# A gated delta rule layer in a four-layer trunk: decays by ScalarE, masks and key scaling moved in the queues, sums of squares by TensorE

## The chip, the cores and the metric

The kernel runs on one core of a Trainium2 chip. The metric is the device time of one execution in microseconds, from the launch of the program to its end. Before the change it was 1247.69 us, the median of three runs (1246.97 to 1249.37).

Five engines work side by side, each with a queue of its own that it serves in order: TensorE (PE, matrix products; its weight loads are listed as PEld), VectorE (DVE), ScalarE (ACT), GpSimd (POOL) and SyncE (SP), which here only issues transfers. Products land in PSUM, in banks of 128 rows by 512 numbers; everything else lives in SBUF, 128 partitions wide.

## What is computed

The reference is a decoder trunk of four layers for one sequence of 256 tokens with 1024 features. Every layer is `x += mixer(rmsnorm(x)); x += conv_ffn(rmsnorm(x))`. The mixers are, in order, block-sparse attention, a short gated convolution, a gated delta rule and attention again. The change touches the third alone, with 8 heads of 128. In short:

```python
qkv = silu(causal_dwconv(proj[..., :3 * d], conv_w))
q, k = l2norm(q) * dh ** -0.5, l2norm(k)
gc = cumsum(g)                                 # g <= 0, so gc only falls
decay = where(i >= j, exp(gc[i] - gc[j]), 0)
a_mat = where(i > j, (k_beta @ k.T) * decay, 0)
t_mat = inverse(a_mat + eye)                   # unit lower triangular
u, w = t_mat @ v_beta, t_mat @ (k_beta * exp(gc))
attn = where(i >= j, (q @ k.T) * decay, 0)
v_new = u - w @ state
o = (q * exp(gc)) @ state + attn @ v_new
state = state * exp(g_last) + (k * exp(g_last - gc)).T @ v_new
```

The reference cuts the sequence into chunks of 64; the kernel uses two chunks of 128 tokens (t = 0 and 1), which is the same in exact arithmetic. Where i >= j the difference gc[i] - gc[j] is minus the distance of the two, so exp(-|gc[i] - gc[j]|) is the decay there, and a number between 0 and 1 on the other side of the diagonal.

## The kernel before

**Weights.** All weights come as one stream of 400 chunks of 512 KB, each eight tiles of 128x128. `Stream` issues a chunk's transfer on SyncE's queue into one of four buffers (wraw, L130); ScalarE rounds it to the high part (whi, L152), VectorE takes the rest (wlo, L153), five chunks ahead of TensorE. A tile's product is three matmuls of 256 columns (xh by whi, xl by whi, xh by wlo). The transfer of a chunk is issued in the program right after the conversion of an earlier one, so SyncE's queue waits wherever a buffer is still to be read.

**The order of TensorE.** It is written by a planner, `Weave`. `fill()` yields the products of the layer job by job (here q0 to q7, one query and one key tile of a head each, then values and gates), and beside it steps are registered: generators that yield `(cost, wait)`. The planner keeps a time t of its own; it advances by the cost of what is emitted, and a step goes on when its wait, a number or a named event with a lag, is past. All the lags are constants (L_QK = 6.0, L_BLOCKS = 6.0, L_JOIN = 13.0 and so on, in the planner's microseconds). TensorE's instructions stay in the order in which the planner emits them. The other engines' queues are ordered by a scheduler that estimates when each instruction can run; `after(inst)` pins an instruction behind the TensorE instruction emitted last.

**The delta rule layer** (`gdn`). The heads are two halves of four; half 0 is ready first. In the program's order:

- `gates` makes g, its running sum gc (L665), and calls `decays` for both halves. `decays` (L681) gets gc[i] in every row by TensorE into a bank of PSUM, subtracts gc[j] and adds a mask of 0 or -1e30 on VectorE (L692, 16 times 128x128), and takes exp of the whole on ScalarE (L696, twice 128x1024): s.dt.
- `queries_keys` (L699) is there for each head: VectorE scales the job's bank (u, L702), ScalarE makes the first tap of the convolution (L420) and VectorE the other three (L422), each for the query and the key, and ScalarE the silu (L707).
- `lengths` (L711), for each head of a half: TensorE transposes query and key of both chunks into one bank (four transposes, L257), ScalarE copies the key's first chunk out (kt, L724) and squares all four out of the bank, each with a sum along the row (jk, L729). Then few-column work on VectorE and GpSimd makes the factors rn, sk and sw, and VectorE scales kt (L742).
- `systems` (L745): TensorE multiplies key by key and key by query, VectorE multiplies with sk and s.dt into aq (L758, two for each head). SyncE stores the key part in DRAM (L766), and VectorE makes am, aq with the off-diagonal 16-blocks alone (L772).
- `invert` (L775): SyncE gathers the diagonal 16x16 blocks (bl, L781), GpSimd inverts them by elimination, 28 small instructions in a row (L792, L794), SyncE stores the result (L796) and gathers it back in another layout (xc, L799); VectorE makes xt32 (xt, L802).
- `join16` and `join_half` put the inverse together from the 16-blocks: a transpose on VectorE (xi, L809), products with am, and so on up to 128. Then the states and outputs of the two chunks follow (`half`, L940).

"Group" below means TensorE's instructions of one head in `lengths`; "key product" means a head's two products in `systems`.

## Time and profile before

| what | before |
|---|---|
| median of three runs | 1247.69 us (1246.97 to 1249.37) |
| the profiled execution, device time | 1247.2 us |
| its span in the trace | 1245.1 us |
| TensorE busy | 1225.7 us (98% of the span) |
| VectorE busy | 982.9 us (79%) |
| ScalarE busy | 775.5 us (62%) |
| GpSimd busy | 104.4 us (8%) |
| mean granted TensorE clock | 0.994 |

The span runs from the first to the last profiled instruction; 2.1 us of the execution lie around it. Times of single instructions and stretches are microseconds from the start of the span. A row of the timeline gives start, duration (of all that are merged in it), engine, source line, operation, and what it writes and reads, with the idle time before it and who ended that. Instructions of one engine overlap at their ends, so the distance from start to start is what a queue pays. The granted clock is 1.00 at 2.4 GHz and 0.50 at 1.2 GHz. The delta rule layer lies between about 581 and 755 us.

### The profile page before, as it was taken

How to read it: one execution, taken by the hardware profiler on the slowest of the kernel's cores; microseconds unless marked ns; L12 is line 12 of the kernel's file. 1: busy time of each engine (PE TensorE's matmuls, PEld its weight loads, DVE VectorE, ACT ScalarE, POOL GpSimd, SP SyncE). 2: the span in 40 equal slices, each digit the busy share in tenths (PEclk: the TensorE clock that was granted, in tenths of full speed). 3: DMA queues.
4: the chain of work that ended last, by engine and by line, in shares of the span. 5: the costliest groups of instructions: out<-in, count | busy, mean ns of one | idle time of the engine just before them, and what ended most of it. 6: DMA issues, size and time to landing. Idle time of an engine off the chain costs nothing.

```text
span 1245.1 us, 22068 instructions
## 1 busy us (share of the span) xinstructions
PE 1225.7 (98%) x8366; PEld 1127.5 (91%) x8366; DVE 982.9 (79%) x1720; ACT 775.5 (62%) x1427; POOL 104.4 (8%) x147
## 2 busy tenths in 40 slices
PE   9999999999999999999997999999999999999997
PEld 8989988889999988889997999988889989988886
DVE  6756999966878999866995668999775756999952
ACT  6655777644445777645873666777554655777641
POOL 2002000001002000001045102000011002000000
PEclk9999999999999999999998999999999999999998
DMA  8544465655555465655344244555655444466650
GB/s 289 200 153 166 146 201 186 213 188 189 176 182 186 153 201 193 200 189 183 126 131 126 90 136 137 200 192 189 208 190 175 156 161 165 145 202 188 211 177 34
DMA packets 67418, 215.80 MB, mean 173 GB/s; under 512 B 11248, under 2 KB 14832, under 8 KB 67312
## 3 DMA queue, kind: packets, MB, share of 16 engines
q1 hardware_dynamic: 67024, 213.86, 52.3%
q8 instruction: 66, 1.08, 0.3%
q10 hardware_dynamic: 288, 0.52, 0.1%
q14 instruction: 40, 0.33, 0.1%
HBM read 212.13 MB, written 2.23 MB: 172 GB/s over the span
## 4 chain that ended last, share of the span: by engine, by line
PE 89%; DVE 4%; ACT 2%; DMA 2%; issue 1%; POOL 1%; SPq 0%; POOLq 0%; DVEq 0%; ACTq 0%
PE mm L254 72%; PE sm L254 16%; DVE wlo L153 2%; DMA wraw<-wstream 1%; PE sm L257 1%; DVE xl L292 1%; ACT whi L152 1%; DVE yqk L422 1%; POOL xb L794 1%; POOL xm L792 1%; ACT jk L729 0%; DMA bl<-d 0%; DVE x L392 0%; DVE big L692 0%; DMA xc<-d 0%
## 5 line engine op out<-in xcount | busy, mean ns | idle before, releaser
L153 DVE TENSOR_TENSOR wlo<-wraw,whi 128x1024 fp32r<-128x1024 f32 (+1 forms) x404 | 489.5, 1212 | 155.7 <-ACT whi L152 154.0
L152 ACT CAST whi<-wraw 128x1024 fp32r<-128x1024 f32 (+1 forms) x404 | 420.2, 1041 | 290.9 <-PE mm L254 239.5
L254 PE MATMUL mm<-xh,whi 128*128 128x256 f32 x1024 | 296.5, 290 | 0.2 <-ACT whi L152 0.2
L254 PE MATMUL mm<-xh,wlo 128*128 128x256 f32 x1024 | 289.1, 282 | 1.2 <-DVE wlo L153 1.2
L254 PE MATMUL mm<-xl,whi 128*128 128x256 f32 x1024 | 288.7, 282 | 0.7 <-DVE xl L292 0.7
L254 PE MATMUL mm<-xs,whi 128*128 128x512 f32 x704 | 248.3, 394 | 0.0
L254 PE MATMUL mm<-aw,whi 128*128 128x512 f32 x704 | 247.3, 393 | 0.0
L254 PE MATMUL mm<-aw,wlo 128*128 128x256 f32 x704 | 199.1, 283 | 0.0
L254 PE MATMUL mm<-xs,wlo 128*128 128x256 f32 x704 | 199.1, 283 | 0.0
L254 PEld LDWEIGHTS mm<-xh,wlo 128*128 128x128 f32 x1024 | 193.5, 189 | 2.3 <-DVE wlo L153 2.1
L254 PEld LDWEIGHTS mm<-xl,whi 128*128 128x128 f32 x1024 | 193.8, 189 | 1.8 <-DVE xl L292 1.1
L254 PEld LDWEIGHTS mm<-xh,whi 128*128 128x128 f32 x1024 | 193.7, 189 | 1.4 <-ACT whi L152 0.4
L254 PEld LDWEIGHTS mm<-aw,whi 128*128 128x128 f32 x704 | 132.2, 188 | 30.6
L254 PEld LDWEIGHTS mm<-xs,whi 128*128 128x128 f32 x704 | 132.2, 188 | 30.5
L422 DVE SCALAR_TENSOR_TENSOR y<-u,pv,y 128x255 f32<-128x255 f32 (+1 forms) x352 | 149.0, 478 | 0.4
L254 PE MATMUL sm<-xs,whi 128*128 128x512 f32 x384 | 135.7, 393 | 0.0
L306 POOL TENSOR_TENSOR sq<-sq 128x256 f32<-128x256 f32 x62 | 53.3, 859 | 974.6 <-ACT sq L304 972.8
L254 PEld LDWEIGHTS mm<-xs,wlo 128*128 128x128 f32 x704 | 132.4, 188 | 0.0
L254 PEld LDWEIGHTS mm<-aw,wlo 128*128 128x128 f32 x704 | 132.3, 188 | 0.0
L254 PE MATMUL sm<-xs,wlo 128*128 128x256 f32 x384 | 108.6, 283 | 0.0
L420 ACT ACTIVATE y<-u,pv 128x256 f32<-128x256 f32 x176 | 81.4, 504 | 11.9 <-DVE u L451 6.6
L254 PEld LDWEIGHTS sm<-xs,whi 128*128 128x128 f32 x384 | 72.1, 188 | 16.6
(210 smaller groups left out, 1509.5 us busy)
## 6 DMA issues: line engine op xcount, KB each, us to landing
wraw<-wstream SPq DMA_DIRECT2D x396, 512.0 KB, 3.4
wraw<-wstream SPq DMA_DIRECT2D x8, 256.0 KB, 4.8
x<-xT SPq DMA_DIRECT2D x8, 128.0 KB, 4.7
d<-aq SPq DMA_DIRECT2D x2, 512.0 KB, 3.7
out<-xg ACTq DMA_DIRECT2D x2, 256.0 KB, 2.5
cs<-cst SPq DMA_DIRECT2D x1, 329.0 KB, 6.4
pv<-pvec SPq DMA_DIRECT2D x1, 324.5 KB, 4.9
cs<-cst SPq DMA_DIRECT2D x1, 320.0 KB, 5.9
```

What stands on the lines that cost most here:

```text
L152: self.nc.scalar.copy(hi[:, s], raw[:, s])
L153: self.nc.vector.tensor_sub(lo[:, s], raw[:, s], hi[:, s].bitcast(F32))
L254: self.last = nc.tensor.matmul(*a, **k)
L257: self.last = nc.tensor.transpose(*a, **k)
L292: V.scalar_tensor_tensor(xl[n], xn, col(gain + n), xh[n].bitcast(F32), op0=ALU.mult, op1=ALU.subtract)
L306: G.tensor_add(sums[0], sums[0], sq)
L420: S.activation(y, u, AF.Copy, scale=col(taps[0]))
L422: V.scalar_tensor_tensor(y[:, d:], u[:, :T - d], col(c), y[:, d:], op0=ALU.mult, op1=ALU.add)
L792: G.tensor_mul(xm[:, :n, :r], xb[:, :n, k:k + 1].to_broadcast([NS * nb, n, r]), bl[:, k:k + 1, k + 1:].to_broadcast([NS * nb, n, r]))
L794: G.tensor_sub(xb[:, :n, k + 1:], xb[:, :n, k + 1:], xm[:, :n, :r])
```

## The change

It has four parts, all in `gdn`, and changes of constants that follow from them.

- **Decays.** gc is negated once (ngc, 128x16 on VectorE). ScalarE takes Abs(gc[i] - gc[j]) out of PSUM with ngc as its bias, 16 times 128x128, in place of VectorE's subtraction with the mask, and exp is then taken with scale -1. The mask -1e30 leaves the constants. The decays are no longer 0 above the diagonal.
- **Masks later.** The key scores need no mask of their own, because only blocks below or on the diagonal are read of them. The query scores are multiplied with the 0/1 triangle `tri` (128x8x128) once for each half, in `half`, after `join16`. kt is scaled there too. am is made in `invert`, after the elimination has been emitted, and pinned behind TensorE; the planner's wait of 13.0 there is split in 8.5 (L_MASK) and 4.5.
- **Lengths.** `queries_keys` squares the finished silu on ScalarE (128x512). A group is one transpose, of the key's first chunk, and four products of a 128x128 tile of squares with a column of ones, into columns of the same bank. ScalarE copies kt and the four sums out. The planner's cost of a group is 0.4 instead of 0.22.

```diff
-                        V.scalar_tensor_tensor(s.dt[:, a, t, :], pd[:, q * P:(q + 1) * P],
-                                               gc[:, t, s.h0 + a:s.h0 + a + 1], cs[:, C_NEG:C_NEG + P],
-                                               op0=ALU.subtract, op1=ALU.add)
+                        S.activation(s.dt[:, a, t, :], pd[:, q * P:(q + 1) * P], AF.Abs,
+                                     bias=ngc[:, t, s.h0 + a:s.h0 + a + 1])
                     yield 0.9, 0
-                S.activation(s.dt, s.dt, AF.Exp)
+                S.activation(s.dt, s.dt, AF.Exp, scale=-1.0)
...
                 halves[h // G_H].y.append(y)
+                sq = pool.tile([P, 2, T], F32, name="m4", bufs=6)
+                S.activation(sq, y, AF.Square)
+                halves[h // G_H].sq.append(sq)
                 wv.set(f"q{h}", L_QK)
...
                     pt = bank("sm")
+                    PE.transpose(pt[:, :P], s.y[a][:, 1, :P], ident)
                     for i in range(4):
                         q, t = divmod(i, 2)
-                        PE.transpose(pt[:, i * P:(i + 1) * P], s.y[a][:, q, t * P:(t + 1) * P], ident)
-                    S.copy(s.kt[:, a, :], pt[:, 2 * P:3 * P])
-                    for i in range(4):
-                        q, t = divmod(i, 2)
-                        m = 2 * a + t
-                        jk = pool.tile([P, P], F32, name="jk", bufs=1)
-                        S.activation(jk, pt[:, i * P:(i + 1) * P], AF.Square, accum_out=sm[:, q, m:m + 1])
-                    yield 0.22, L_LEN
+                        PE.matmul(pt[:, P + i:P + i + 1], lhsT=s.sq[a][:, q, t * P:(t + 1) * P], rhs=ones[:, 0:1],
+                                  start=True, stop=True)
+                    S.copy(s.kt[:, a, :], pt[:, :P])
+                    S.copy(sm[:, :, 2 * a:2 * a + 2], pt[:, P:P + 4].rearrange("p (q t) -> p q t", q=2))
+                    yield 0.4, L_LEN
...
-                V.tensor_mul(s.kt, s.kt, sw.unsqueeze(2).to_broadcast([P, G_H, P]))
+                s.sw = sw
...
-                s.am = big()
-                V.tensor_mul(s.am, s.aq[:, :, 1, :],
-                             cs[:, C_UP:C_UP + P].unsqueeze(1).to_broadcast([P, NS, P]))
...
+                yield 0, L_MASK
+
+                s.am = big()
+                after(V.tensor_mul(s.am, s.aq[:, :, 1, :],
+                                   cs[:, C_UP:C_UP + P].unsqueeze(1).to_broadcast([P, NS, P])))
...
                 yield from join16(s)
+                after(V.tensor_mul(s.kt, s.kt, s.sw.unsqueeze(2).to_broadcast([P, G_H, P])))
+
+                after(V.tensor_mul(s.aq[:, :, 0, :], s.aq[:, :, 0, :], tri.unsqueeze(1).to_broadcast([P, NS, P])))
```

**Where the queues change.** On TensorE the groups and key products move by a few products: 84 matmuls of the weight stream stand between the first group and the last key product of half 0 where 90 stood, and 180 between that and the join where 174 stood. The three places that follow matter further on.

ScalarE, before, around the silu of head 4 (the second L707 row shown is head 4; jk,sums are the squares with their sums):

```order
L707 ACTIVATE yqk<-yqk 128x512
L729 ACTIVATE jk,sums<-sm 128x128 x2
L420 ACTIVATE yqk<-u,pv 128x256
L729 ACTIVATE jk,sums<-sm 128x128
L420 ACTIVATE yqk<-u,pv 128x256
L729 ACTIVATE jk,sums<-sm 128x128
```

ScalarE, after, from the copies of head 3's group on (m is the tile of squares; the silu is head 4's, the taps L418 are head 5's, the copies at the end are head 4's):

```order
L729 COPY kt<-sm 128x128
L730 COPY sums<-sm 128x2x2
L150 CAST whi<-wraw 128x1024
L707 ACTIVATE yqk<-yqk 128x512
L418 ACTIVATE yqk<-u,pv 128x256
L710 ACTIVATE m_7033<-yqk 128x512
L418 ACTIVATE yqk<-u,pv 128x256
L729 COPY kt<-sm 128x128
L730 COPY sums<-sm 128x2x2
```

Head 4's group on TensorE followed its silu directly; now a tap of head 5 and the square stand between.

VectorE, before, the convolution of head 4 and the scaling of head 5's bank (the second u):

```order
L702 TENSOR_TENSOR u<-mm,rb 128x512
L153 TENSOR_TENSOR wlo<-wraw,whi 128x1024
L422 SCALAR_TENSOR_TENSOR yqk<-u,pv,yqk 128x255 x2
L422 SCALAR_TENSOR_TENSOR yqk<-u,pv,yqk 128x254 x2
L422 SCALAR_TENSOR_TENSOR yqk<-u,pv,yqk 128x253 x2
L153 TENSOR_TENSOR wlo<-wraw,whi 128x1024
L702 TENSOR_TENSOR u<-mm,rb 128x512
```

VectorE, after, the same place:

```order
L420 SCALAR_TENSOR_TENSOR yqk<-u,pv,yqk 128x255
L420 SCALAR_TENSOR_TENSOR yqk<-u,pv,yqk 128x253
L420 SCALAR_TENSOR_TENSOR yqk<-u,pv,yqk 128x254
L702 TENSOR_TENSOR u<-mm,rb 128x512
L420 SCALAR_TENSOR_TENSOR yqk<-u,pv,yqk 128x253
L151 TENSOR_TENSOR wlo<-wraw,whi 128x1024 x2
```

The scaling of head 5's bank, which waits for the last product of job q5, has moved ahead of the last step of head 4's convolution.

VectorE, before, where the gathered inverses of half 0 arrive (xt, xi; aq are score tiles of half 1, big<-aq,cs is am of half 1):

```order
L995 TENSOR_TENSOR z<-mm,rb 128x512
L153 TENSOR_TENSOR wlo<-wraw,whi 128x1024
L758 SCALAR_TENSOR_TENSOR aq<-sm,sk,big 128x256 x2
L802 TENSOR_TENSOR xt_7417<-xc,cs 128x256
L809 STREAM_TRANSPOSE xi_7610<-xt_7417 128x256
L758 SCALAR_TENSOR_TENSOR aq<-sm,sk,big 128x256 x2
L772 TENSOR_TENSOR big<-aq,cs 128x1024
```

VectorE, after, the same place (big<-aq,cs is now am of half 0):

```order
L759 SCALAR_TENSOR_TENSOR aq<-sm,sk,big 128x256 x4
L800 TENSOR_TENSOR big<-aq,cs 128x1024
L1000 TENSOR_TENSOR z<-mm,rb 128x512
L759 SCALAR_TENSOR_TENSOR aq<-sm,sk,big 128x256 x2
L151 TENSOR_TENSOR wlo<-wraw,whi 128x1024
L804 TENSOR_TENSOR xt_7523<-xc,cs 128x256
L759 SCALAR_TENSOR_TENSOR aq<-sm,sk,big 128x256 x2
L811 STREAM_TRANSPOSE xi_7578<-xt_7523 128x256
```

am of half 0 has moved from behind the first store to a place ahead of xt, and the last two score tiles of half 1 from behind xi to a place ahead of it.

SyncE, after, the transfers of half 0 (d is the store in DRAM, bl the gathered blocks); before, no chunk stood between the first two:

```order
L767 DMA d_7240<-aq 128x8x128
L128 DMA wraw<-wstream 128x1024
L778 DMA bl<-d_7240 64x16x16
L128 DMA wraw<-wstream 128x1024 x2
L793 DMA d_7386<-xb 64x256
```

One of the three chunks that followed the gather stands ahead of it now.

## Rows read from the trace of the kernel before

**Rows 1.** The page, busy microseconds, share of the span and instructions of each engine:

```profile
PE 1225.7 (98%) x8366; PEld 1127.5 (91%) x8366; DVE 982.9 (79%) x1720; ACT 775.5 (62%) x1427; POOL 104.4 (8%) x147
```

**Rows 2.** TensorE's waits, 585 to 775 us: total, times, longest.

```profile
PE sm L254 <- DVE xi L809: 5.7, 2, 5.1
PE sm L257 <- ACT yqk L707: 1.0, 1, 1.0
...
PE sm L257 <- ACT jk L729: 0.3, 1, 0.3
```

**Rows 3.** Microsecond windows, first and last of six: engines' busy, then clock, DMA share, GB/s.

```profile
664.00:665.00 1.00, 0.82 (x4) 0.85 (x5) 0.97 (x4) 0.00 (x0) 0.00 (x0) 0.50 1.01 406
...
669.00:670.00 1.00, 1.00 (x6) 1.00 (x6) 1.00 (x2) 0.00 (x0) 0.00 (x0) 0.50 0.00 0
```

**Rows 4.** The chain that ended last, 600 to 670 us: start, duration, what.

```profile
631.46 1.42 PE mm L254 x12
...
633.78 0.89 DVE aq L758 x2
634.68 2.93 DMA d<-aq
637.63 4.68 DMA bl<-d
...
658.05 1.96 DMA d<-xb
...
663.59 0.46 DVE xi L809
```

**Rows 5.** TensorE's timeline at a norm's sums and at head 0's four transposes.

```profile
20.62 0.50 PE L254 MATMUL sm<-cs,sq 128*128 128x1 f32 x4
20.99 0.36 PE L254 MATMUL mm<-xh,whi 128*128 128x256 f32 x1
...
615.10 0.60 PE L257 MATMUL sm<-cs,yqk 128*128 128x128 f32 x4
615.45 0.36 PE L254 MATMUL mm<-xh,whi 128*128 128x256 f32 x1
```

**Rows 6.** Groups by line and shape, 585 to 775 us: busy, mean ns, idle before.

```profile
L729 ACT ACTIVATE jk<-sm 128x128 f32<-128x128 f32 x32 | 8.9, 279 | 0.5
...
L420 ACT ACTIVATE yqk<-u,pv 128x256 f32<-128x256 f32 x16 | 7.4, 499 | 2.7 <-DVE u L702 2.7
...
L422 DVE SCALAR_TENSOR_TENSOR yqk<-u,pv,yqk 128x253 f32<-128x253 f32 x16 | 7.0, 476 | 0.0
...
L702 DVE TENSOR_TENSOR u<-mm,rb 128x512 f32<-128x512 f32 x8 | 5.5, 684 | 2.6 <-ACT rb L339 2.6
...
L707 ACT ACTIVATE yqk<-yqk 128x512 f32<-128x512 f32 x8 | 5.1, 634 | 1.8 <-DVE yqk L422 1.5 <-DVE gc L665 0.3
...
L895 ACT ACTIVATE big<-sm,rn 128x128 f32<-128x128 f32 x16 | 4.6, 368 | 0.6 <-PE sm L257 0.6
...
L692 DVE SCALAR_TENSOR_TENSOR big<-sm,gc,cs 128x128 f32<-128x128 f32 x16 | 4.3, 342 | 0.0
```

**Rows 7.** Timeline of GpSimd's elimination in half 0, and VectorE's instruction beside it.

```profile
650.58 0.36 POOL L792 TENSOR_TENSOR xm<-xb,bl 64x63 f32<-64x63 f32 x1
651.02 1.33 POOL L794 TENSOR_TENSOR xb<-xb,xm 64x63 f32<-64x63 f32 x1
...
650.96 1.21 DVE L153 TENSOR_TENSOR wlo<-wraw,whi 128x1024 fp32r<-128x1024 f32 x1
```

**Rows 8.** The page, issues of the weight stream: count, size, us to landing.

```profile
wraw<-wstream SPq DMA_DIRECT2D x396, 512.0 KB, 3.4
```

**Rows 9.** Half 1's chain in the timeline: its store, its xi, TensorE's use.

```profile
664.82 0.38 SPq L766 DMA_DIRECT2D d<-aq  x1
...
692.54 0.45 DVE L809 STREAM_TRANSPOSE xi<-xt 128x256 f32<-128x256 f32 x1
...
693.82 1.85 PE L254 MATMUL sm<-xi,big 128*128 128x16 f32 x16
```

More of the change, by code (lines that the diff above doesn't have):

```diff
@@ L41 @@
 L_HEAD, L_SOFTMAX, L_TURN, L_MIX, L_READY = 3.5, 9.0, 1.0, 2.5, 0.5
-L_QK, L_V, L_LEN, L_SYS, L_BLOCKS, L_JOIN, L_XI, L_PM, L_OUT = 6.0, 6.0, 1.0, 0.5, 6.0, 13.0, 1.0, 2.5, 1.0
+L_QK, L_V, L_LEN, L_SYS, L_BLOCKS, L_MASK, L_JOIN, L_XI, L_PM, L_OUT = 6.0, 6.0, 1.0, 0.5, 6.0, 8.5, 4.5, 1.0, 2.5, 1.0
 PV_MIX = 0
@@ L58 @@
 C_TRI = C_BASE + 3 * P
-C_NEG = C_TRI + P
-C_BD = C_NEG + P
+C_BD = C_TRI + P
 C_LV = C_BD + P
@@ L77, in constants @@
     c[:, C_TRI:C_TRI + P] = i[:, None] <= i[None, :]
-    c[:, C_NEG:C_NEG + P] = np.where(i[None, :] >= i[:, None], 0.0, -1e30)
     c[:, C_ST:C_ST + 2 * H] = i[:, None] % (2 * H) == np.arange(2 * H)[None, :]
@@ L618, in gdn @@
             neg = pool.tile([P, H], F32, name="neg")
+            ngc = pool.tile([P, 2, H], F32, name="ngc")
             yh, yl = {}, {}
@@ L665, in gates @@
                 V.tensor_copy(gc.rearrange("p a b -> p (a b)"), pg[:, :3 * H])
+                V.tensor_scalar(ngc, gc[:, :2], -1.0, None, op0=ALU.mult)
                 V.tensor_sub(dl, gc[:, 2, :], gc[:, 0, :])
@@ L678, in __init__ @@
                 def __init__(self, h0):
-                    self.h0, self.y = h0, []
+                    self.h0, self.y, self.sq = h0, [], []
             def decays(s):
```

## The prediction

> **What bounds the kernel now.** I read the busy times first, then TensorE's waits in the stretch of the delta rule layer, then the chain that ended last there, then single instructions. TensorE is busy in 98% of the span [rows 1], so a change can only pay where TensorE waits, and whatever it adds to TensorE's queue is paid in full unless it falls into such a wait. From 585 to 775 us the waits are few [rows 2]: 5.1 us for xi, the start of the join in the first half of the heads (half 0), 1.0 us for the silu of a query/key pair, 0.3 us for a bank that ScalarE was still reading. Behind the long wait the granted clock is 0.50 in each of the six microseconds from 664 to 670 [rows 3], that is 1.2 instead of 2.4 GHz, so about 3.0 us of full-speed work are lost there as well. The long wait ends a chain of transfers and GpSimd work [rows 4]: the last two score tiles aq at 633.78, their store at 634.68, the gather of the diagonal blocks at 637.63, GpSimd's elimination, the store of the inverses at 658.05, the gather back, then xt and its transpose xi, which ends at 664.05. That is 29.4 us from the first store. TensorE resumes at 664.18 and had run dry at 664.18 - 5.1 = 659.1. What the change is worth is therefore decided by two numbers: when the first store is issued, and how long that chain is, against what TensorE has to do meanwhile.
>
> **TensorE's own work.** A head's four transposes become one transpose and four products with a single column. The trace has that product: the layer norms' sums, 128x1, where two products are four instructions and the next product starts 0.37 us later (20.62 to 20.99) [rows 5], 0.0925 us each. Four transposes hold the queue for 0.35 us (615.10 to 615.45) [rows 5]. A head's group is nine instructions afterwards, 9 x 0.0925 = 0.83 us, so 0.48 us more, and 3.8 us for eight heads. Six of the groups stand ahead of the last key product of half 0 (2.9 us), two between it and the join (1.0 us). Nothing hides them, since this queue is full in between.
> The Trainium skill (TensorE: Matmul & The Clock Gate, Back-to-back issue gap) gives about 81 ns per pair of weight load and matmul of 128 columns as the sustained rate; by that the five extra instructions of each group would cost an estimated 3.2 us in all. The rows have the very form, so 3.8 us stays in the sum.
>
> **The wait at head 4.** The single-column products read squares that ScalarE now makes from the finished silu. For head 4 the rows of the order show the path: VectorE multiplies out head 5's projection (u) before the last convolution step of head 4, then ScalarE has silu, one tap of head 5, the square. Head 5's projection ends six products after head 3's group; from there the path is 0.68 + 0.48 + 0.63 + 0.50 + 0.63 = 2.9 us by mean durations [rows 6]. TensorE has six products left until it needs the square, 0.7 us (twelve are 1.42 us [rows 4]). It waits 2.2 us where it waited 1.0, so 1.2 us more. The 0.3 us wait for a bank goes, because the 32 squares from PSUM go that held it, and six products have moved behind the last key product, 0.7 us. The first store is issued later by 2.9 + 1.2 - 0.3 - 0.7 = 3.1 us.
>
> **What VectorE and ScalarE gain.** The 16 subtractions leave VectorE (4.3 us [rows 6]), the squares leave ScalarE (8.9 us, and the reads of their sums [rows 6]); ScalarE gets 16 Abs and 8 squares of 128x512. The trace has no Abs with a column as bias out of PSUM; between the square of a bank, 0.28 us, and the copy with a column as scale, 0.37 us, both 128x128 [rows 6], I take 0.30, near the pipelined ones, 4.8 us in all (4.5 to 5.9). The eight squares are 8 x 0.63 = 5.1 us by the silu of the same tile [rows 6]. ScalarE ends with less to do. All this buys nothing by itself: in rows 4 the first store waits for aq, which follows TensorE's last key product and not VectorE's backlog, and that product has moved later. The cover of the Abs is TensorE's work up to head 3; at 0.37 us each, head 3's square would come about 1 us after its turn and the first store later by that. Negating gc, the small copies of sums and the smaller constant cost nothing that TensorE waits for.
>
> **The chain of half 0.** VectorE's order now puts the last two score tiles of half 1 between xt and xi; two of them take 0.89 us [rows 4], so xi comes 0.9 us later after the first store. Key scaling leaves GpSimd's stretch and the masked copy am enters it. The price of that is in the trace: GpSimd's step on 64x63 takes 0.36 us alone and 1.33 us when VectorE's 1.21 us subtraction starts with it [rows 7], a push of 1.0 us; am for kt is 0 to +0.5 us, I take 0. On SyncE's queue one weight chunk now stands between the store and the gather of the blocks. It waits for a buffer that VectorE frees about 2 us after the store was issued, and the gather has to wait for the store to land anyway (2.93 us [rows 4]); its packets may stand behind the chunk's 3.4 us [rows 8]. I take 0 and keep +3.4 us as the end above; below, 2.0 us of the gather's 4.68 [rows 4] may go, if the three chunks that shared it before were its delay. So xi is at +3.1 + 0.9 = +4.0 us against before, and TensorE resumes at about 668.2. It runs dry at 659.1 + 3.8 + 1.2 - 0.3 = 663.8, so the wait is still 4.4 us, and I let the clock fall as it did before.
>
> **Half 1 and the sum.** Its first store follows its last score tiles, which stand ahead of xi now: +4.0 - 0.45 = +3.5 us on 664.82, where 0.45 is xi's own time [rows 9]. Its chain was ready at 692.99 and was used at 693.82 [rows 9], a slack of 0.8 us. Key scaling, the mask of the queries' scores and am of half 1 now lie in its GpSimd stretch: three more VectorE instructions of two SBUF tensors, 0.0 to 2.5 us together by rows 7. TensorE itself comes at +4.0, the chain at +3.5 - 0.8 + 1.2 = +3.9 with the middle of that; no new wait beyond a few tenths. Behind it TensorE has no long wait in which the shift could vanish. The profiled execution took 1247.2 us (1245.1 span, 2.1 around it), 0.5 below the median of the three runs. 1247.2 + 4.0 is 1251.2; I take 1251.0, since means count overlapping starts twice on the path of head 4.
> The Trainium skill (SBUF — State Buffer, SBUF: two separate sides) says that a VectorE instruction with two SBUF inputs and a GpSimd one that reads SBUF exclude each other for the whole instruction. Rows 7 agree to 0.2 us. By the page the three would push 0.7 + 1.2 + 1.2 = 3.1 us, an estimate, and half 1 would end the sum at +5.8 us.
>
> **The rivals.** (1) The same, within 0.2%: the wait of half 0 is short enough, or falls so, that the clock stays up, which saves 3.0 us on TensorE, and half 1's chain is not pushed: TensorE then comes at +1.0 and the chain at +2.7. The later of the two counts, 1249.9; with 2.0 us off the gather it is +0.7, 1247.9. I take 1249. For it: the wait shrinks by my own sum; against: two conditions at once. (2) Faster: the chain of half 0 is shorter than the time between the new first store (637.8) and TensorE running dry (663.8), 26.0 us instead of 29.4 + 0.9. The gather would have to lose 2.0 us and GpSimd two of its pushes of 1.0 with it, and xi would not wait for the two score tiles. Then 5.1 of wait and 3.0 of clock go against 3.8 + 1.2 - 0.3 of added work: -3.4 us, 1243.8. Rows 4 show no such gather, so this is unlikely. (3) Slower still: the gather stands behind the weight chunk for its whole 3.4 us, or half 1's chain takes the full pushes: 1254.4. Everything then waits, in both halves. (4) The change doesn't do what it says: if the planner's group of 0.4 for what takes 0.83 left the products in places where their banks are not free, single waits appear at each head; nothing in the order shows a bank reused sooner, and I fold it into (3).
>
> **How the numbers follow.** Forecast near 1251: 0.42. (3) with (4): 0.18. (1): 0.31. (2): 0.09. The range reaches from the lower end of (1), less half a microsecond for the runs' own spread, to (3): 1247.3 to 1254.5; that leaves out (2) and half of the tail above. A measurement of this kernel tells 0.2% or 2.5 us from no change. Slower by more than that begins at 1250.2; the forecast lies 0.8 above it, so a part of its own spread falls within: slower 0.58, same 0.33, faster 0.09.
>
> **What would show it.** Right: TensorE's nine instructions of a head at some 0.8 us; a wait of about 2 us for ScalarE's square at head 4; the first store near 637.8; a wait of 4 to 5 us for xi near 664 with the clock at one half behind it; GpSimd's steps of half 1 with more of 1.2 us and over. Wrong: no wait for xi; a first store before 635; the single-column products at half the price; or a gather of blocks that lands 2 us sooner or later than 4.7 us after its issue.

## The result

The changed kernel takes 1258.37 us (median of 4 runs, 1255.83 to 1260.11) beside 1248.21 us before: a ratio of 1.008, 95% interval 1.006 to 1.010. A second set of runs (6, beside 29 of before) gave 1256.31 us, ratio 1.0071, 1.0055 to 1.0086. So it is slower by 8 to 10 us, where the forecast had 3.3 and the range ended at 1254.5. The ten runs scatter over 1254.1 to 1260.5, wider than those of before. Three runs, one of e5 and two of e6, took 1492 to 4281 us; the medians below count them and the ratios do not.

The profiled execution of the first set was its slowest, 1260.11 us; the second set's profile is of a run of 1255.48 us. I read both. Lines of source differ a little from those of before: L252 is the product, L255 the transpose, L759 aq, L811 the turn to xi.

TensorE of the changed kernel (the page, engines), to hold against [rows 1]:

```profile
PE 1236.2 (98%) x8406; PEld 1137.8 (90%) x8406; DVE 982.1 (78%) x1707; ACT 774.6 (62%) x1395; POOL 110.0 (9%) x147
```

Its waits from 585 to 785 us (total, times, longest), first profile:

```profile
PE sm L252 <- DVE xi L811: 7.9, 2, 4.4
PE sm L255 <- ACT yqk L707: 1.2, 1, 1.2
PE sm L252 <- ACT m L909: 1.1, 1, 1.1
PE sm L252 <- ACT m L710: 0.6, 1, 0.6
```

and of the second profile:

```profile
PE sm L252 <- DVE xi L811: 4.8, 2, 3.1
PE sm L255 <- ACT yqk L707: 1.2, 1, 1.2
```

[Rows 2] had one long wait of 5.1 us. Now the first xi is waited for 3.45 and 3.13 us, and the second xi, which came 0.8 us early before, 4.41 and 1.64 us. The waits alone don't make 10 us. The granted clock falls too. Windows of a microsecond of the first profile (share busy, then, from the right, GB/s, DMA share, clock), at head 4 and at the second join:

```profile
627.00:628.00 1.00, 0.85 (x8) 0.85 (x8) 1.00 (x4) 0.50 (x2) 0.11 (x1) 0.99 0.44 70
628.00:629.00 1.00, 1.00 (x6) 1.00 (x7) 1.00 (x5) 0.67 (x3) 1.00 (x1) 0.50 0.90 336
...
631.00:632.00 1.00, 1.00 (x8) 0.91 (x7) 0.47 (x2) 0.00 (x0) 0.61 (x1) 0.80 0.16 66
...
698.00:699.00 1.00, 0.00 (x0) 0.00 (x0) 0.00 (x0) 0.44 (x1) 0.00 (x0) 1.00 0.90 293
...
700.00:701.00 1.00, 0.00 (x0) 0.00 (x0) 0.00 (x0) 0.00 (x0) 0.00 (x0) 0.50 0.92 289
...
705.00:706.00 1.00, 1.00 (x6) 1.00 (x6) 0.30 (x1) 0.00 (x0) 0.00 (x0) 0.50 0.00 0
...
709.00:710.00 1.00, 1.00 (x7) 1.00 (x6) 1.00 (x2) 0.67 (x3) 0.00 (x0) 0.55 0.00 0
```

In the profile of before, the clock fell once in the layer, at 664 to 670 us [rows 3]. In both profiles of the changed kernel it falls three times: behind the waits of head 4, at the first join, and at the second. A part of these stretches lies in the waits themselves (700 to 701 us above); in the rest TensorE is busy, at 1.2 instead of 2.4 GHz.

**Where the time went.** I take the layer from the last square that GpSimd adds for the norm before it to the first for the norm behind it. The rest of the program differs by 1.4 us or less between these three profiles. One row a kernel gives the layer's length, then TensorE's busy time; the clock is the third number from the right. Before:

```profile
580.57:749.89 169.32, 161.49 (x1456) 157.93 (x1455) 124.16 (x232) 109.89 (x252) 38.22 (x71) 0.98 0.40 125
```

after, first profile:

```profile
580.67:763.44 182.77, 172.03 (x1495) 168.14 (x1494) 122.76 (x219) 109.34 (x220) 44.20 (x70) 0.94 0.36 116
```

after, second profile:

```profile
579.59:758.84 179.25, 171.61 (x1495) 167.71 (x1494) 122.90 (x219) 109.34 (x220) 41.59 (x70) 0.95 0.36 119
```

Busy time times (1 - clock), summed over windows of half a microsecond, is what the lower clock took (lost). What is left of the busy time is work at full speed.

| us | layer | TensorE idle | lost to the clock | work |
|---|---|---|---|---|
| before | 169.3 | 7.8 | 3.2 | 158.3 |
| after, first profile | 182.8 | 10.7 | 8.9 | 163.2 |
| after, second profile | 179.3 | 7.6 | 8.5 | 163.1 |
| e13, head 4 filled | 176.4 | 6.0 | 5.8 | 164.6 |
| e14, head 4 and joins filled | 174.8 | 2.5 | 0.0 | 172.3 |

In the second profile the work is up by 4.8 us, the idle time is no longer than before, and 5.3 us more are lost to the clock. The first has 2.9 us of idle time on top.

The work hardly changes from run to run, but the clock does, and the profile of before is a favourable one. Its mean granted clock is 0.994; of the 108 runs of the kernel before that stand beside the experiments only 17 have that, and their mean is 0.992. The ten runs of the changed kernel have 0.991. One minus the clock, times the span, is 9.9 us in the mean of the runs before and 11.7 in that of the changed kernel (waits included; a clock is listed to 0.001, which is 1.2 us of a single run). By the runs the clock thus takes about 2 us more than before and not 5; beyond the 4.8 us of work, the remaining 2 us or so would be waits.

### The profile page after: what moved, and what is told of

The parts are those of the page before. It is cut to its first block, busy times and chain, and to the rows that moved or that the text cites. A ratio compares the mean times of both kernels' runs of the same rounds, so it can differ in the third digit from the quotient of the medians.

```text
span 1258.3 us, 22108 instructions
## 1 busy us (share of the span) xinstructions
PE 1236.2 (98%) x8406; PEld 1137.8 (90%) x8406; DVE 982.1 (78%) x1707; ACT 774.6 (62%) x1395; POOL 110.0 (9%) x147
## 4 chain that ended last, share of the span: by engine, by line
PE 90%; DMA 3%; DVE 2%; POOL 2%; issue 2%; ACT 1%; SPq 0%; POOLq 0%; DVEq 0%; ACTq 0%
PE mm L252 73%; PE sm L252 16%; POOL xb L791 1%; POOL xm L789 1%; DVE wlo L151 1%; DMA d<-aq 1%; DVE xl L290 1%; PE sm L255 1%; DMA xc<-d 1%; DMA bl<-d 0%; DMA x<-xT 0%; DMA d<-xb 0%; DVE x L390 0%; ACT whi L150 0%; POOL xb L786 0%
## 5 line engine op out<-in xcount | busy, mean ns | idle before, releaser
L252 PE MATMUL mm<-xh,whi 128*128 128x256 f32 x1024 | 297.6, 291 | 0.5 <-ACT whi L150 0.5
L252 PE MATMUL mm<-xh,wlo 128*128 128x256 f32 x1024 | 289.4, 283 | 0.8 <-DVE wlo L151 0.8
L252 PE MATMUL mm<-xl,whi 128*128 128x256 f32 x1024 | 289.3, 282 | 0.4 <-DVE xl L290 0.4
L252 PE MATMUL mm<-xs,whi 128*128 128x512 f32 x704 | 248.3, 394 | 0.0
L252 PE MATMUL mm<-aw,whi 128*128 128x512 f32 x704 | 247.3, 393 | 0.0
L252 PE MATMUL mm<-aw,wlo 128*128 128x256 f32 x704 | 199.1, 283 | 0.0
L252 PE MATMUL mm<-xs,wlo 128*128 128x256 f32 x704 | 199.1, 283 | 0.0
L252 PEld LDWEIGHTS mm<-xh,whi 128*128 128x128 f32 x1024 | 194.7, 190 | 2.1 <-ACT whi L150 1.1
L252 PEld LDWEIGHTS mm<-xl,whi 128*128 128x128 f32 x1024 | 194.6, 190 | 1.7 <-DVE xl L290 0.8
L252 PEld LDWEIGHTS mm<-xh,wlo 128*128 128x128 f32 x1024 | 194.1, 190 | 1.5 <-DVE wlo L151 1.4
L252 PEld LDWEIGHTS mm<-aw,whi 128*128 128x128 f32 x704 | 132.2, 188 | 30.6
L252 PEld LDWEIGHTS mm<-xs,whi 128*128 128x128 f32 x704 | 132.2, 188 | 30.5
L252 PE MATMUL sm<-xs,whi 128*128 128x512 f32 x384 | 135.7, 393 | 0.0
L252 PEld LDWEIGHTS mm<-xs,wlo 128*128 128x128 f32 x704 | 132.4, 188 | 0.0
L252 PEld LDWEIGHTS mm<-aw,wlo 128*128 128x128 f32 x704 | 132.3, 188 | 0.0
L252 PE MATMUL sm<-xs,wlo 128*128 128x256 f32 x384 | 108.6, 283 | 0.0
L418 ACT ACTIVATE y<-u,pv 128x256 f32<-128x256 f32 x176 | 81.4, 504 | 12.9 <-DVE u L449 7.1
L252 PEld LDWEIGHTS sm<-xs,whi 128*128 128x128 f32 x384 | 72.1, 188 | 16.6
```

What stands on the lines that cost most here:

```text
L252: self.last = nc.tensor.matmul(*a, **k)
L418: S.activation(y, u, AF.Copy, scale=col(taps[0]))
```

## The experiments

Eighteen kernels ran. Ratios are to the kernel before, with their 95% intervals; 0.1% is 1.25 us.

### The parts alone

Theory M: the late masks hold up GpSimd in half 1, and that is most of it. Rival L: the lengths do it all.

e1 is the kernel before with the masks and the key scaling late.

> The kernel before with the mask part of the change alone: key scaling, the queries' mask and am made late, the wait of 13.0 split. Lengths and decays as before. Theory M (the three late VectorE products stretch GpSimd's elimination of half 1, and TensorE then waits for xi of half 1 and its clock falls): GpSimd's elimination of half 1 takes 16 to 18 us where it took 14.1, TensorE waits 2 to 4 us for the second xi near 693 with the clock at 0.50 behind it, and the median is 4 to 8 us over before. Rival L (the lengths' products make the first store late, and all that follows is that delay): no wait for the second xi above 1 us, median within 2 us of before.

e2 has the lengths alone.

> The kernel before with the lengths part alone: squares of the finished silu by ScalarE, one transpose and four one-column products a head. Masks and decays as before. Theory M: the first store some 4 to 5 us later than 634.7, the clock at 0.50 for about 3 us behind the waits of head 4, TensorE's extra products 3.8 us; GpSimd's elimination of half 1 stays at 14 to 15 us and the second xi makes no wait over 1 us; median 3 to 6 us over before. Rival L: median 8 to 11 us over before, with the wait at the second xi of 4 us that the changed kernel has.

e3 is the changed kernel with the lengths as before.

> The changed kernel with the lengths as before (four transposes a head, ScalarE's squares with sums out of PSUM): decays and masks are the change's. Theory M: like the kernel with the masks alone, 4 to 8 us over before, since the decays by Abs move no wait of TensorE: the two within 1 us of each other. Rival L: within 2 us of before. If the decays matter by themselves, this one and the masks alone differ by 2 us or more.

e4 takes the masks out of GpSimd's stretch (kt in `lengths` and am behind the store again, the queries' mask behind both joins):

```diff
-                s.sw = sw
+                V.tensor_mul(s.kt, s.kt, sw.unsqueeze(2).to_broadcast([P, G_H, P]))
...
+                s.am = big()
...
                 yield from join_half(s, 64, (0,), (), ...)
+                after(V.tensor_mul(s.aq[:, :, 0, :], s.aq[:, :, 0, :], tri.unsqueeze(1).to_broadcast([P, NS, P])))
```

> The changed kernel with am and the key scaling where they were before, and the queries' mask moved behind both joins of a half, so that at most one of the three VectorE products lies beside GpSimd's elimination of half 1; one wait of 13.0 again. Lengths and decays stay the change's. Theory M: the elimination of half 1 at 14 to 15.5 us, the wait for the second xi under 1.5 us, its clock dip gone, median 1251 to 1254 (3 to 6 over before). Rival L: the elimination may be shorter but the wait for the second xi stays over 3 us, median 1256 to 1260.

e5 is the kernel before with the 16 Abs and, as they need it, the queries' mask at the place that it has in e4.

> The kernel before with the decays by Abs on ScalarE alone; the queries' mask, which they need, is multiplied in behind both joins of a half, where no GpSimd work of the half lies beside it. Theory M2 (the 16 Abs, 0.41 us as issued but some 0.25 us apart, stand in ScalarE's queue just when it is full, so the squares of the heads come about 2 us later and TensorE waits for them): the first store 1.5 to 2.5 us later than before measured from the layer's start, median 1250.5 to 1253 (2 to 4 over before). Rival (ScalarE has room, as the prediction held): first store within 0.5 us, median within 1 us of before.

| kernel | median, us | ratio | interval |
|---|---|---|---|
| e1 masks alone | 1251.79 | 1.0026 | 1.0016 to 1.0037 |
| e2 lengths alone | 1253.57 | 1.0042 | 1.0029 to 1.0055 |
| e5 decays alone | 1249.52 | 1.0007 | 0.9999 to 1.0016 |
| e3 masks and decays | 1255.08 | 1.0055 | 1.0042 to 1.0067 |
| e4 lengths, decays, one mask | 1256.58 | 1.0062 | 1.0046 to 1.0077 |

The three parts add up to 0.75%, 9.4 us, about the whole. Both theories were wrong as stated. Masks alone cost 3.3 us, not 4 to 8, so M has at most a third, though its mechanism is there: in e1 the second xi is waited for 2.6 us, with the clock at one half behind it. The lengths cost 5.2 us, as M had it (3 to 6), and not 8 to 11, so L has about half. e4 removed GpSimd's hold-ups as meant (elimination of half 1 13.2 us, second xi waited for 1.0 us), yet it gained at most 1 to 2 us on the changed kernel, which the intervals don't tell from nothing, and not 4 to 7. e3 is 0.3% above e1, more than the decays cost alone. By the two profiles it waits 1.1 us longer for the second xi and loses 2.0 us more to the clock; why the decays bring that here and not alone I can't say. ScalarE's queue, though, shows what the decays do. In e5, sixteen Abs run from 607.58 to 612.76 with one exp between:

```profile
607.58 2.42 ACT L694 ACTIVATE big<-sm,ngc 128x128 f32<-128x128 f32 x9
609.84 1.11 ACT L697 ACTIVATE big<-big 128x1024 f32<-128x1024 f32 x1
610.79 1.97 ACT L694 ACTIVATE big<-sm,ngc 128x128 f32<-128x128 f32 x7
```

and TensorE waits later for squares (its waits in e5, 580 to 770 us):

```profile
PE sm L254 <- DVE xi L810: 4.1, 2, 3.7
PE sm L254 <- ACT jk L730: 1.9, 3, 1.2
...
PE sm L257 <- ACT jk L730: 0.5, 1, 0.5
```

The first store is 1.9 us later (56.0 us behind the layer's start, 54.1 before), but the wait for the first xi is 1.4 us shorter, and little is left in the total.

### The price of a late product beside GpSimd

Products of the queries' scores with the 0/1 triangle were added to the kernel before. Its scores are masked already, so nothing changes in what is computed. e10 has one, e11 three, e12 three in the other half (`!=`):

```diff
                 yield from join16(s)
+                for _ in range(3 if s.h0 == 0 else 0):
+                    after(V.tensor_mul(s.aq[:, :, 0, :], s.aq[:, :, 0, :], tri.unsqueeze(1).to_broadcast([P, NS, P])))
```

> The kernel before with one product of the queries' scores with the 0/1 triangle added on VectorE behind the second turn of half 0's join, where the change has it. The scores are masked already, so it changes nothing that is computed. Theory M (a VectorE product of two SBUF tensors holds up GpSimd's step for as long as it runs): GpSimd's elimination of half 1 at 14.8 to 15.4 us where it took 14.1, the second xi 0.7 to 1.3 us later against its store, median 0 to 2.5 us over before. Rival (only VectorE's own time counts): elimination at 13 to 14.3 us, median within 1 us.

> The same with three such products in a row. Theory M: the elimination of half 1 at 16.5 to 17.5 us, a wait for the second xi of 1.5 to 3 us with the clock at 0.50 behind it, median 2.5 to 6 us over before. Rival: elimination under 14.5 us, no wait for the second xi above 1 us, median within 1.5 us of before.

> The same three products at the same place of half 1's join in place of half 0's, where no GpSimd elimination is left to hold up. Theory M: elimination of half 1 at 13 to 14.5 us as before, median within 1.5 us of before. Rival (VectorE's added 3.7 us themselves are what delays the join): 2 to 5 us over before here too.

VectorE's three products in e11, and GpSimd's steps of the time:

```profile
680.53 1.32 DVE L948 TENSOR_TENSOR aq<-aq,cs 128x1024 f32<-128x1024 f32 x1
...
682.97 1.30 DVE L948 TENSOR_TENSOR aq<-aq,cs 128x1024 f32<-128x1024 f32 x1
...
686.41 1.22 DVE L948 TENSOR_TENSOR aq<-aq,cs 128x1024 f32<-128x1024 f32 x1
...
680.84 1.13 POOL L792 TENSOR_TENSOR xm<-xb,bl 64x48 f32<-64x48 f32 x1
682.04 1.15 POOL L794 TENSOR_TENSOR xb<-xb,xm 64x48 f32<-64x48 f32 x1
683.27 1.11 POOL L792 TENSOR_TENSOR xm<-xb,bl 64x39 f32<-64x39 f32 x1
```

Each step takes about 0.3 us alone and 1.1 beside a product (the step at 682.04 lies beside a subtraction of the weight stream, which also reads two SBUF tensors), and the third product came after the elimination had ended. From the landing of its blocks, half 1's elimination takes 13.2, 14.0 and 14.9 us in e12, e10 and e11, with 3, 4 and 5 such long steps: 0.9 us each, near [rows 7]. By the Trainium skill (SBUF — State Buffer, SBUF: two separate sides) a VectorE instruction with two SBUF inputs and a GpSimd one that reads SBUF exclude each other for a whole instruction; the rows agree. But the added products don't set the count alone: the kernel before has 4 long steps and 14.1 us without any, since three of VectorE's subtractions fall on steps there and two in e12. So neither e10 (14.8 to 15.4 expected) nor e11 (16.5 to 17.5) grew as theory M had it.

The times don't follow that dose: 1.0010 (1.0001 to 1.0018), 1.0013 (1.0005 to 1.0022), and 1.0012 (1.0004 to 1.0021) where the three stand in the other half and hold up nothing. So M's mechanism is real, but no time here follows it; the second xi was still ready when TensorE came to it. What e11 did not have is the late store of the changed kernel. What the three profiles do share is a second fall of the clock, 1.7 us lost, behind a wait of 0.84 us for another tile. The kernel before has the same wait, and in its profile no fall; first its rows, then those of e10:

```profile
681.04 0.69 PE L254 MATMUL sm<-xt,m 32*32 32x32 f32 x16 [0.84 <-ACT big L866]
...
683.00:684.00 1.00, 1.00 (x11) 1.00 (x10) 0.23 (x1) 0.84 (x3) 0.76 (x4) 1.00 0.02 8
```

```profile
681.39 0.73 PE L254 MATMUL sm<-xt,m 32*32 32x32 f32 x16 [0.84 <-ACT big L866]
...
683.00:684.00 1.00, 1.00 (x6) 1.00 (x6) 0.00 (x0) 0.80 (x4) 0.80 (x3) 0.50 0.00 0
```

### The clock

Theory C: a wait costs more than itself, because the clock is at one half behind it. It was tested with products that nobody reads, put into the waits. Ahead of the joins, in e7 (e6 has 20 and 0):

```diff
                 yield 0, L_XI
+                pf = bank("sm")
+                for _ in range(14 if s.h0 == 0 else 18):
+                    PE.matmul(pf[:, :P], lhsT=ident, rhs=s.y[0][:, 0, :P], start=True, stop=True)
                 pp = bank("sm")
```

> The kernel before with 20 products of 128x128 that nobody reads put on TensorE's queue directly ahead of the join of half 0, about 4.6 us of work in its wait of 5.1 us. Theory C (the clock falls because TensorE stands idle there, and that loss of some 3.3 us comes on top of the wait): the wait for xi shrinks to under 1 us, the clock stays at 1.00 from 664 to 671, median 1244.5 to 1246.5 (2 to 4 under before). Rival (the clock falls there for another reason, or the wait is what costs and not the clock): clock at 0.50 all the same, median 1248 to 1250.

> The changed kernel with 14 and 18 such products that nobody reads ahead of the join of half 0 and of half 1, about 3.2 and 4.2 us, in its waits of 3.5 and 4.4 us. Theory C: both clock dips go, 3.2 and 3.9 us, and the median falls from 1258.4 to 1250 to 1253. Rival: the dips stay and the median stays at 1257 to 1259.

On the changed kernel the time came as expected: 1252.04 us, 1.0041 (1.0024 to 1.0058), though the kernel has 7 us more to do. Of the two falls only the first went; the profile, of its second slowest run, still waits 2.5 us for the second xi and loses 1.7 us behind it. On the kernel before the theory failed: 1248.41, 1.0001 (0.9992 to 1.0010). There the wait went as planned (0.34 us left), but the clock fell all the same, later and for a shorter time, with TensorE fully busy:

```profile
664.00:665.00 1.00, 1.00 (x12) 1.00 (x11) 1.00 (x2) 0.00 (x0) 0.00 (x0) 1.00 1.05 385
...
666.00:667.00 1.00, 1.00 (x8) 1.00 (x7) 1.00 (x2) 0.00 (x0) 0.00 (x0) 0.57 1.11 352
667.00:668.00 1.00, 1.00 (x6) 1.00 (x6) 0.33 (x1) 0.00 (x0) 0.00 (x0) 0.50 1.21 380
```

It fell again behind a new wait of 1.8 us for the second xi. 4.6 us of added work bought 4.3 us of waits and no clock.

e9 is the changed kernel again.

> The changed kernel itself once more, for a second profile and more runs: its first profile was of its slowest run. If the three falls of the clock that it showed (behind head 4's square, behind the first and behind the second xi) are what every execution has, the median is again 1257 to 1260 and the second profile has all three. If they come and go, single runs scatter over 1253 to 1260 in steps of 1.5 to 4 us and the second profile lacks one.

It came out between the two cases. The median was 1256.31, the runs scatter over 6 us, and the second profile has all three falls, of other lengths: at head 4 some seven microseconds from the first row below to the last, where the first profile had three and a half, at the second join three and a half where it had ten, waits included.

```profile
626.00:627.00 1.00, 0.93 (x6) 0.93 (x6) 1.00 (x4) 0.42 (x2) 0.19 (x1) 0.70 0.37 90
...
633.00:634.00 1.00, 1.00 (x7) 0.92 (x6) 0.30 (x1) 0.76 (x1) 0.00 (x0) 0.88 0.00 0
```

e13 fills head 4 alone; the columns written are unused ones of the group's own bank:

```diff
+                    if s.h0 + a == 4:
+                        for _ in range(7):
+                            PE.matmul(pt[:, 2 * P:3 * P], lhsT=ident, rhs=halves[0].y[0][:, 0, :P], start=True, stop=True)
                     PE.transpose(pt[:, :P], s.y[a][:, 1, :P], ident)
```

> The changed kernel with 7 products of 128x128 that nobody reads, some 1.6 us, on TensorE's queue ahead of head 4's group, in its waits of 1.2 and 0.6 us. Theory C2 (what the prediction missed is the granted clock: a wait of TensorE that the sum counts once brings a fall to one half behind it, 1.7 or 3.4 us more): no fall of the clock between 626 and 634, first store 1.5 to 3.5 us earlier than in the two profiles of the changed kernel (58.9 and 60.5 after the layer's start), median 1254 to 1256.5 where these had 1256.3 and 1258.4. Rival (the fall there follows the one-column products and not the wait): clock at 0.50 there all the same and median at 1257 or over.

1253.49 us, 1.0037 (1.0025 to 1.0049), clear of both sets of the changed kernel: 1.6 us of useless work took 4 to 5 us off. The other engines' queues are in the changed kernel's order, and TensorE's differs by these products alone. TensorE's timeline at head 4, and two windows with the clock behind it:

```profile
623.91 1.73 PE L252 MATMUL sm<-yqk,cs 128*128 128x128 f32 x14
625.47 0.27 PE L255 MATMUL sm<-cs,yqk 128*128 128x128 f32 x1
626.18 1.05 PE L252 MATMUL sm<-cs,m 128*128 128x1 f32 x8 [0.44 <-ACT m L710]
```

```profile
628.00:629.00 1.00, 1.00 (x8) 0.89 (x7) 1.00 (x4) 0.55 (x1) 1.00 (x2) 1.00 0.89 254
...
630.00:631.00 1.00, 1.00 (x8) 0.92 (x7) 1.00 (x2) 0.75 (x1) 0.64 (x1) 1.00 0.27 111
```

The one-column products are all there and the clock stays at 1.00, so they alone don't bring the fall. The first store came 57.3 us behind the layer's start, against 58.9 and 60.5.

e14 fills all three places.

> The same together with the 14 and 18 products ahead of the two joins that took the changed kernel to 1252.0. Theory C2: median 1249.5 to 1251.5, lost clock in the layer under 3.5 us where the changed kernel has 8.5 to 8.9. Rival: no further gain over 1252.

1251.95 us, 1.0031 (1.0020 to 1.0042), within the interval of e13 and no faster than e7, as the rival had it. In e6, e7 and e14 some instructions of other queues moved too (in e7 and e14 half 1's gather back of the inverses stands one chunk earlier on SyncE's), so they are weaker evidence than e13. In the profile of e14 the layer has no fall at all:

```profile
580.00:754.20 174.20, 171.70 (x1569) 168.11 (x1568) 122.00 (x218) 108.97 (x220) 40.39 (x71) 1.00 0.38 121
```

39 products at 0.22 us are 8.6 us of added work, and the layer is still 4.5 and 8.0 us shorter than in the two profiles of the changed kernel. Its ten runs show the clock's price once more: the six with a mean granted clock of 0.998 took 1250.5 to 1252.3 us, the three with 0.995 1253.7 to 1256.8. One thing stays open: e4's profile has the same two waits at head 4, 1.19 and 0.59 us, and no fall behind them:

```profile
625.24 0.33 PE L255 MATMUL sm<-cs,yqk 128*128 128x128 f32 x1 [1.19 <-ACT yqk L707]
626.16 1.05 PE L252 MATMUL sm<-cs,m 128*128 128x1 f32 x8 [0.59 <-ACT m L710]
...
629.00:630.00 1.00, 1.00 (x11) 1.00 (x10) 1.00 (x3) 0.00 (x0) 1.00 (x1) 1.00 0.67 258
```

So a wait of that size may bring a fall or not, and no run here tells which.

### The order of the joins, and the queue of the transfers

e8 raises the planner's wait ahead of half 0's join by 4.5, on the kernel before.

> The kernel before with the planner's wait ahead of the join of half 0 raised by 4.5, so that 30 more matmuls of the weight stream (3.6 us) stand ahead of it and as many fewer between it and the join of half 1. If the first wait is free to be filled with work: the wait for the first xi falls to 1.5 us, median 1241 to 1245. If the second join is as tight as its slack of 0.8 us says: the wait turns up at the second xi, 3 to 6 us near 690, with the clock's fall behind it, and the median is 1247 to 1250.

1253.85 us, 1.0046 (1.0034 to 1.0058): worse than both expected cases, but the second case in kind. The wait moved to the second xi (5.5 us). Half 1's store was issued at 660.94 behind half 0's gather back and three chunks, and its own gather only at 669.57, 8.6 us later (4.4 before).

e15 and e16 have the other three transfers of a half issued by GpSimd (`nc.gpsimd.dma_start` in `invert`), on the kernel before and on the changed one.

> The kernel before with the gather of the blocks, the store of the inverses and the gather back issued by GpSimd, the engine that waits for them, and not in SyncE's queue between chunks of the weight stream. Theory Q (the gathers and stores stand behind weight chunks in one queue): both chains 1 to 4 us shorter from first store to xi, median 1244 to 1247.5. Rival (the transfers' own time and GpSimd's issuing are what they take): chains as long or up to 3 us longer, median 1248 to 1252.

> The changed kernel with the same three transfers issued by GpSimd. Theory Q: half 1's chain from store to xi, 33.1 us in the first profile and 30.1 in the second against 28.2 before, comes to 27 to 29 us, the second wait under 1.5 us, median 1251 to 1255. Rival: no shorter chain, median 1256 to 1260.

1248.83 us, 0.9999 (0.9990 to 1.0008), and 1256.04 us, 1.0053 (1.0037 to 1.0069). Theory Q falls: the chain from half 1's store to xi takes 28.5 and 29.8 us, and in the kernel before, which SyncE serves, it took 28.2.

e17 and e18 put the two together.

> The kernel before with GpSimd issuing the three transfers of a half and the planner's wait ahead of half 0's join raised by 4.5. With the later join alone half 1's store stood behind half 0's gather in SyncE's queue and landed 8.6 us after its issue, and the second xi was waited for 5.5 us. If that queue was the obstacle: half 1's store at 658, its gather issued by 663 to 664, the second wait under 1.5 us and the first under 3, median 1242 to 1246 (2.5 to 6 under before). If half 1's chain takes as long in any case, the second wait stays at 4 to 6 us and the median is 1250 to 1254.

> The same with the wait raised by 2.5, so that fewer products move ahead of the first join. If the queue was the obstacle: median 1243 to 1247, both waits under 3 us. If not: first wait 4 to 5 us, second 2 to 4 us, median 1248 to 1252.

e17: 1247.16 us, 0.9990 (0.9981 to 0.9999). e18: 1252.33 us, 1.0029 (1.0017 to 1.0041). In e17 nothing is waited for at the second xi any more:

```profile
PE sm L254 <- DVE xi L809: 3.7, 1, 3.7
PE sm L257 <- DVE m L931: 1.7, 1, 1.7
```

Of the eighteen it is the only one whose whole interval lies below 1, by 1.2 us in the middle and only just; 2.5 to 6 had been expected. With a step of 2.5 in place of 4.5 TensorE waits 7.8 us in all for the two transposes of half 0's join. A gain that turns over with one constant is not one to build on.

## Why the prediction was wrong

- **TensorE's own work: right in kind, a fifth too small.** A group starts at 615.20 and the next product at 616.12, 0.92 us and not 0.83 (timeline of the changed kernel):

```profile
615.20 0.27 PE L255 MATMUL sm<-cs,yqk 128*128 128x128 f32 x1
615.31 0.95 PE L252 MATMUL sm<-cs,m 128*128 128x1 f32 x8
616.12 0.36 PE L252 MATMUL mm<-xh,whi 128*128 128x256 f32 x1
```

  That is 0.57 us more a head, 4.6 for eight, where the sum had 3.8; an instruction with one column takes 0.10 us here and took 0.0925 in [rows 5]. The Trainium skill's 81 ns for a pair of 128 columns (TensorE: Matmul & The Clock Gate, Back-to-back issue gap) had given an estimate of 3.2 us, which was further off.
- **Head 4's wait: nearly right.** The sum had 2.2 us of waiting, all of it for the square, in place of 1.0; the rows show 1.19 for the silu and 0.59 for the square. The first store was to be 3.1 us later; where the clock did not fall it is 3.2 (57.3 against 54.1 us behind the layer's start, e4 and e13).
- **The clock behind the new waits: left out.** This is the step that failed. The prediction says "I let the clock fall as it did before", at the first join, and its sum counts the longer wait at head 4 once. In both profiles two new falls came, at head 4 (1.7 and 3.4 us lost) and at the second join (3.9 and 1.7). With the first join's, 3.2 and 3.4, these are the 8.9 and 8.5 us of the table against 3.2. e13 prices the first of them by times and not only by profiles: with 1.6 us of useless work, no fall at head 4 in its profile and every queue as it was otherwise, it takes 4 to 5 us less, about half of the slowdown. Part of that is the fall itself and part what follows from it, since the first store is late by 1.6 to 3.2 us more with it (58.9 and 60.5 against 57.3), and the second xi is then waited for 4.41 and 1.64 us and not 0.25. What e13 is still over before, 4.6 us, is not far from the forecast, though its profile also holds the useless work and two falls (5.8 us lost). What stays open is how the clock of the two kernels compares: the profiles say 5.3 to 5.7 us more, the clocks of all runs about 2, and no run here has the kernel before without a fall. So it is in part luck that the sum with one more line, 4.0 + 5.3 = 9.3 us, lies between the 8.4 and 10.2 us that the two sets of runs gave.
- **The chain of half 0: near.** xi comes 1.1 us behind xt (667.57 and 668.70), as the order had it. The gather took 3.3 us and not 4.7, so most of the lower end that I kept for it came true, and the wait is 3.1 to 3.5 us where I had 4.4.
- **Half 1: "no new wait beyond a few tenths" was wrong.** Slack 0.8, chain +3.9: the store did come nearly as forecast (668.8 against 664.8, +4.0 where I had +3.5), but its gather was issued 6.0 us behind it (4.4 before) and the elimination took 17.8 and 15.1 us (14.1). VectorE's and GpSimd's rows of the first profile, with two of the late products:

```profile
683.80 1.31 DVE L951 TENSOR_TENSOR aq<-aq,cs 128x1024 f32<-128x1024 f32 x1
...
692.50 1.25 DVE L800 TENSOR_TENSOR big<-aq,cs 128x1024 f32<-128x1024 f32 x1
...
684.11 1.17 POOL L789 TENSOR_TENSOR xm<-xb,bl 64x63 f32<-64x63 f32 x1
...
692.74 1.12 POOL L791 TENSOR_TENSOR xb<-xb,xm 64x28 f32<-64x28 f32 x1
```

  I had kept 0.0 to 2.5 us for the three and took 1.2; 1.0 to 3.7 came. In the first profile 6 steps are long where 4 were, and 1.0 of the 3.7 us lies ahead of the first step. In the second profile only 4 steps are long, yet gather and elimination together still made 1.6 us of wait.
- **The decays: nearly right.** They were costed at nothing and came to 0.9 us alone, with an interval that holds zero. The Abs starts every 0.25 us, below the 0.30 that I took. But the first store was not untouched: in e5 it is 1.9 us later, which the sum had only for a slower Abs.
- **The rivals.** The slower one (1254.4) had one right place, half 1, and one right mechanism, GpSimd's pushes, but no rival had a second fall of the clock, though [rows 3] showed what one costs.

## What to carry to other kernels

Where TensorE is nearly always busy, a new wait on it may cost more than itself: look at what the trace shows behind the waits that are there. In the two profiles of the changed kernel the falls behind waits lost 1.7 to 3.9 us each, and e4 had the same two waits at head 4 without a fall, so such a line is a risk to be given a chance, not a fixed price. One profile is one execution: compare its granted clock with that of the other runs before a few microseconds are put down to the clock. A short stretch of useless products in a wait can tell whether the clock or the wait is what costs, if all other queues keep their order, as in e13.

## What the runs showed of the hardware

The clock fell in e6 with TensorE busy from 663.2 us on and a wait of 0.34 us ahead of it, and did not fall in e4 behind waits of 1.19 and 0.59 us; behind the same wait of 0.84 us it fell in e10 and not in the profile of the kernel before. So neither the presence nor the length of one wait decided it. Single falls lost between 1.5 and 4.8 us. An instruction with one column costs TensorE as much queue time (0.10 us, and a product has two of them) as a transpose of 128 columns (0.09 us, four in 0.35 before). A GpSimd step of 0.3 us takes 1.1 beside a VectorE instruction that reads two SBUF tensors. And the 64 KB transfers gave no shorter chain from GpSimd's queue than from SyncE's (28.5 us from half 1's store to xi in e15, 28.2 before).
